# Softmax without division in an encoder layer: wide probabilities, and reciprocal sums multiplied into the gate

## The chip, the cores and the metric

The kernel runs on one core of a Trainium2 chip. The metric is the device time of one execution in microseconds. The core has five engines with an instruction queue each: TensorE (PE in the profile; PEld is its loading of weights), VectorE (DVE), ScalarE (ACT), GpSimd (POOL) and SyncE (SP). Every queue is worked off in order, and an instruction that waits holds up all that stand behind it. Transfers (DMAs) are issued by an instruction in one of the queues and then carried out by 16 DMA engines.

## The reference

One encoder layer on a sequence of 4096 tokens with 1024 channels: an input projection, windowed attention and a pooling branch, an output projection, and a normalised residual. Cut to what matters here:

```python
proj = jnp.einsum('bsd,de->bse', rmsnorm(x, pre_norm_g[l]), w_in[l])
q, k, v, g_a, u_p, g_p = jnp.split(proj, splits, axis=-1)
# banded_attention: blocks of 128 queries, keys of the block and of its two neighbours
s = jnp.where(valid, einsum(q, k) * scale + bias, NEG)
m = jnp.maximum(jnp.max(s, axis=-1, keepdims=True), sk)        # sk: one learned sink per head
p = jnp.exp(s - m)
p = p / (jnp.sum(p, axis=-1, keepdims=True) + jnp.exp(sk - m))
o = jnp.einsum('bnkgqs,bnskd->bnqkgd', p.astype(v.dtype), vw)
a = o * jax.nn.silu(g_a)
mixed = jnp.einsum('bse,ed->bsd', jnp.concatenate([a, pool], axis=-1), w_out[l])
x = x + rmsnorm(mixed, post_norm_g[l])
```

There are 8 query heads of 64 channels and 2 groups of keys and values. The division by the row sum can stand before the product with the values, or behind it.

## The kernel before, in words

Every float32 operand of a large product is carried as a pair of float16 numbers, a high part and a rest, and a product is three matmuls. The first stage (up to some 500 us of the span) projects the gates and the pooling branch and writes what the second stage needs to DRAM (`x_scr`, `ga_scr`, `yp_scr`, `w_scr`). The second stage is the attention with the output projection. It goes through the 32 blocks of 128 queries from the last to the first, in pairs: a unit `u` is the pair of blocks 2u + 1 (odd) and 2u (even), 256 tokens.

A block is attended in two halves of four heads. For one half:

- `scores` (L1313): TensorE multiplies queries and keys into two PSUM tiles `s`.
- `logits` (L1336), four times on VectorE: adds the bias, finds the row's minimum of the negated logits (`nm`), writes `p` in float32. GpSimd has put the sinks into one more column of `p` (L1330).
- `exps` (L1347), four times on ScalarE: the exponential over 384 + 1 columns, in place, with the row sum in `den`.
- `denominators` (L1354, L1357) on VectorE: divides the four sums by 2^14 and takes the reciprocals `rd`.
- `probs` (L1369), four times on ScalarE, one head each: the float16 high part of `p * rd`, into `pn`.
- `rests` (L1377), four times on VectorE: `p * rd` less that high part, also into `pn`.
- `turn` (L1386): a transposing DMA, issued by SP, from `pn` to `pt`.

When both halves of a block are turned, `values` (L1483, L1513) multiplies `pt` with the values `vv` on TensorE, `copy_o` (L1543, ScalarE) and `gate` (L1534, L1551, L1555, VectorE) apply a scale and the gate `ga` (loaded by `load_ga`, L1460, into tiles named `gb`), and the gated output `at` goes into the output projection.

That projection is done with seven products for two by two blocks of tokens and channels (`mix_p1` to `mix_p7`, `product` L1676). Their operands are sums and differences of `at` and of the pooling branch `yf` (`sum1` to `sum4`, L1611 to L1620), each split into a high part by ScalarE (`high`, L1578) and a rest by GpSimd (`low`, L1582), into tiles `y..` and `ys..`. Products are combined by VectorE (`add`, L1715), squared by ScalarE for the norm (`square`, L1699, output `jkb`), multiplied by the gain on GpSimd (`gain`, L1710), scaled (`mean`, L1728 and L1733, `residual`, L1737) and stored.

Between these stand the projections of the next unit's keys, values and queries (`project_t`, L1273). `do_q` projects the queries of a unit in two halves, both into the same PSUM bank `acc1`; `keep_q` (L1262 on ScalarE, L1263 on VectorE) copies each away before the bank is used again. Products also use that bank.

The order on every engine is written out by hand: `due(t, f, ...)` puts a step into a plan at a due time, and at the end all steps are issued in the order of their due times, each engine taking its own in that order. For blocks 27 to 2, 13 units, a loop (`for b in reversed(range(2, NB - 4))`) sets the due times; the four blocks before and the two behind have their times in tables (`soft(...)`, `at_(...)`). `softmax(b, half, t)` holds the offsets of the steps above:

```python
        for i in range(4):
            due(t + 0.1 + 0.67 * i, logits, b, half, i)
            due(t + 0.8 + 0.8 * i, exps, b, half, i)
            due(t + 4.5 + 0.6 * i, probs, b, half, i)
            due(t + 5.1 + 0.62 * i, rests, b, half, i)
        due(t + 4.3, denominators, b, half)
        due(t + 7.8, turn, b, half)
```

All DMAs are issued by SP. The DMAs share eight completion semaphores, taken in turn in the order of the plan, and a DMA is not issued before the one that had its semaphore last has landed.

Of the kernel before, what the change touches and what calls it, by code (L numbers as in the profile page):

```python
# [8 lines left out]
F32 = mybir.dt.float32  # L9
# [3 lines left out]
AF = mybir.ActivationFunctionType  # L13
ALU = mybir.AluOpType
# [3 lines left out]
P = 128  # L18
S = 4096
D = 1024  # L20
# [3 lines left out]
NB = S // P  # L24
BPM = T // P
NH = 8
# [27 lines left out]
P_SCALE = 2.0**14  # L54
# [80 lines left out]
def hybrid_layer(ctx: ExitStack, tc, io, out):  # L135
    nc = tc.nc
# [4 lines left out]
    dram = ctx.enter_context(tc.tile_pool(name="dram", bufs=1, space=DRAM))  # L141
    gemm = ctx.enter_context(tc.tile_pool(name="gemm", bufs=1, space=PSUM))

    XB0 = const.tile([P, 8192], F16, name="xb0")
# [35 lines left out]
    x_scr = dram.tile([NU, P, 2, 2, HK, UT], F16, name="x_scr")  # L180
    yp_scr = dram.tile([NB, P, 4, P], F32, name="yp_scr")
    ga_scr = dram.tile([NB, P, 4, P], F32, name="ga_scr")
    wb_scr = dram.tile([6, P, 2, D], F16, name="wb_scr")
    w_scr = dram.tile([8, P, 2, HK, 512], F16, name="w_scr")

# [25 lines left out]
    with ExitStack() as actx:  # L211
# [13 lines left out]
        rows = pa.tile([P, T], F32, name="rows")  # L225
# [728 lines left out]
        b = turn("n2")  # L954
# [322 lines left out]
                n += 1  # L1277

    pt, p_t, nm_t, den_t, rd_t, pn_t = {}, {}, {}, {}, {}, {}

    def keys(b):
        return [kb for kb in range(3) if 0 <= b - 1 + kb < NB]
# [6 lines left out]
    def due(t, fn, *args):  # L1289
        plan.append((t, len(plan), fn, args))  # L1290
# [30 lines left out]
    def logits(b, half, i):  # L1321

        kbs = keys(b)
        nk, lo, j0 = len(kbs) * P, kbs[0] * P, 2 * half
        if i == 0:
            nm_t[b, half] = pb.tile([P, 4], F32, name=f"nm{b}_{half}", tag="nm")
            den_t[b, half] = pb.tile([P, 4], F32, name=f"den{b}_{half}", tag="den")
            rd_t[b, half] = pb.tile([P, 4], F32, name=f"rd{b}_{half}", tag="rd")
            p = p_t[b, half] = pb.tile([P, 4, 3 * P + 1], F32, name=f"p{b}_{half}", tag="p")
            nc.gpsimd.tensor_copy(  # L1330
                p.rearrange("p (g j) k -> p g j k", g=2)[:, :, :, nk],
                nsink.rearrange("p (g j) -> p g j", g=2)[:, :, j0 : j0 + 2],
            )
        jj, gg = divmod(i, 2)
        hh, h = 2 * gg + jj, 4 * gg + j0 + jj
        nc.vector.tensor_tensor_reduce(  # L1336
            out=p_t[b, half][:, hh, :nk], in0=s_t[jj][:, gg, :nk],
            in1=bias[:, h, lo : lo + nk], scale=negc[:, h : h + 1], scalar=nsink[:, h : h + 1],
            op0=ALU.add, op1=ALU.min, accum_out=nm_t[b, half][:, hh : hh + 1],
        )  # L1340

    def exps(b, half, i):
        nk = len(keys(b)) * P
        jj, gg = divmod(i, 2)
        hh = 2 * gg + jj
        p = p_t[b, half]
        nc.scalar.activation(  # L1347
            p[:, hh, : nk + 1], p[:, hh, : nk + 1], AF.Exp, bias=nm_t[b, half][:, hh : hh + 1],
            scale=-1.0, accum_out=den_t[b, half][:, hh : hh + 1],
        )  # L1350

    def denominators(b, half):
        den = den_t.pop((b, half))
        nc.vector.tensor_scalar(  # L1354
            out=den, in0=den, scalar1=1.0 / P_SCALE, scalar2=None, op0=ALU.mult
        )
        nc.vector.reciprocal(rd_t[b, half], den)  # L1357

    def prob_view(b, half):
        nk = len(keys(b)) * P  # L1360
        return pn_t[b, half][:, : 8 * nk].rearrange("p (v h k) -> p v h k", v=2, h=4)

    def probs(b, half, i):
        nk = len(keys(b)) * P
        if i == 0:
            pn_t[b, half] = pb.tile(
                [P, 2 * 4 * 3 * P], F16, name=f"pn{b}_{half}", tag="pn", bufs=PN_BUFS
            )
        nc.scalar.activation(  # L1369
            prob_view(b, half)[:, 0, i], p_t[b, half][:, i, :nk], AF.Copy,  # L1370
            scale=rd_t[b, half][:, i : i + 1],
        )

    def rests(b, half, i):
        nk = len(keys(b)) * P
        pn4 = prob_view(b, half)
        nc.vector.scalar_tensor_tensor(  # L1377
            out=pn4[:, 1, i], in0=p_t[b, half][:, i, :nk], scalar=rd_t[b, half][:, i : i + 1],
            in1=pn4[:, 0, i], op0=ALU.mult, op1=ALU.subtract,
        )  # L1380

    def turn(b, half):
# [6 lines left out]
    def softmax(b, half, t):  # L1389

        for i in range(4):
            due(t + 0.1 + 0.67 * i, logits, b, half, i)
            due(t + 0.8 + 0.8 * i, exps, b, half, i)
            due(t + 4.5 + 0.6 * i, probs, b, half, i)
            due(t + 5.1 + 0.62 * i, rests, b, half, i)
        due(t + 4.3, denominators, b, half)
        due(t + 7.8, turn, b, half)


    kv_t = {}  # L1400
# [347 lines left out]
    def load_gain():  # L1748
        nc.sync.dma_start(
            gpost, io["g_post"].rearrange("(o a) -> o a", o=1).to_broadcast([P, D])  # L1750
        )

    now = [0.0]
    dummy = pb1.tile([P, 1], F32, name="dummy")

# [86 lines left out]
    def at_(t, fn, *args):  # L1842
        due(z + t, fn, *args)

    def soft(b, half, tl, te, td, tp, tr, tt):

        for i in range(4):
            at_(tl + 0.62 * i, logits, b, half, i)
            at_(te + 0.65 * i, exps, b, half, i)
            at_(tp + 0.55 * i, probs, b, half, i)  # L1850
            at_(tr + 0.62 * i, rests, b, half, i)
        at_(td, denominators, b, half)
        at_(tt, turn, b, half)

    def cast(th, tw, u, name, f, eng):
# [337 lines left out]
```

## Time and profile before

| what | before |
|---|---|
| median of 3 runs | 1161.81 us (1161.5 to 1165.42) |
| the profiled execution | 1162.76 us, span 1161.0 us |
| VectorE, ScalarE, GpSimd busy in the span | 947.8, 717.7, 313.7 us |
| HBM read, written | 114.68 MB, 60.34 MB |
| DMA packets | 301683, mean 197 GB/s |

The span runs from the first instruction to the last; the time of an execution holds some 1.8 us more around it. Rows of the timeline give the start, the duration, the engine, the line, the operation and its tiles; `x4` joins four in a row, and square brackets give the idle time ahead of an instruction and who ended it. `PEld` and `PE` overlap. Tile names are those of the code without their numbers. A row of the groups gives a line's engine and operation, its tiles and shapes, the count, the busy time in us and the mean of one in ns.

### The profile page before, as it was taken

How to read it: one execution, taken by the hardware profiler on the slowest of the kernel's cores; microseconds unless marked ns; L12 is line 12 of the kernel's file. 1: busy time of each engine (PE TensorE's matmuls, PEld its weight loads, DVE VectorE, ACT ScalarE, POOL GpSimd, SP SyncE). 2: the span in 40 equal slices, each digit the busy share in tenths (PEclk: the TensorE clock that was granted, in tenths of full speed). 3: DMA queues.
4: the chain of work that ended last, by engine and by line, in shares of the span. 5: the costliest groups of instructions: out<-in, count | busy, mean ns of one | idle time of the engine just before them, and what ended most of it. 6: DMA issues, size and time to landing. Idle time of an engine off the chain costs nothing. (4 is left out here: it accounts for less than half of the span.)

```text
span 1161.0 us, 32325 instructions
## 1 busy us (share of the span) xinstructions
PE 1146.3 (99%) x13420; PEld 873.5 (75%) x13420; DVE 947.8 (82%) x1875; ACT 717.7 (62%) x1485; POOL 313.7 (27%) x310
## 2 busy tenths in 40 slices
PE   8999999999999999999999999999999999999997
PEld 7998888888888888886667676576666767667653
DVE  6889988988799974568878888878887888887886
ACT  6876556536654542257676776676667677667772
POOL 0001120211111010201524433532533443353231
PEclk8999999999999999999999999999999999999999
DMA  9645575867667664299975886788777688777885
GB/s 344 217 128 180 174 259 183 285 229 238 227 190 225 206 179 134 76 289 242 250 185 144 197 211 143 200 202 177 177 196 184 148 198 215 140 196 165 178 216 143
DMA packets 301683, 228.36 MB, mean 197 GB/s; under 512 B 219568, under 2 KB 259504, under 8 KB 296928
## 3 DMA queue, kind: packets, MB, share of 16 engines
q1 hardware_dynamic: 301536, 226.30, 72.5%
q8 instruction: 105, 1.72, 0.6%
q14 instruction: 42, 0.34, 0.1%
HBM read 114.68 MB, written 60.34 MB: 151 GB/s over the span
## 5 line engine op out<-in xcount | busy, mean ns | idle before, releaser
L689 PEld LDWEIGHTS <-wq 128*128 128x128 f16 x4104 | 401.6, 98 | 50.4 <-DVE wq L310 2.6
L689 PE MATMUL y<-xt,wq 128*128 128x256 f16 x1512 | 203.3, 273 | 0.1
L1347 ACT ACTIVATE p<-p,nm 128x385 f32<-128x385 f32 (+1 forms) x256 | 152.9, 599 | 36.5 <-POOL p L1330 20.3
L1273 PE MATMUL aq<-xb,xb 128*128 128x256 f16 x1024 | 173.4, 273 | 0.2 <-DVE mo L1715 0.2
L1273 PEld LDWEIGHTS <-xb 128*128 128x128 f16 x1536 | 150.1, 98 | 26.4 <-issue 8.0
L1676 PE MATMUL ms<-wo,ys 128*128 128x512 f16 x720 | 163.7, 379 | 0.0
L1377 DVE SCALAR_TENSOR_TENSOR pn<-p,rd,pn 128x384 f16<-128x384 f32 (+1 forms) x256 | 157.6, 667 | 5.9 <-ACT pn L1369 5.9
L1336 DVE CUSTOM_DVE_ANT_0 p<-s,nt,nsink 128x384 f32<-128x384 f32 (+1 forms) x256 | 156.0, 666 | 2.0 <-PE s L1313 2.0
L1273 PE MATMUL aq<-xb,xt 128*128 128x256 f16 x512 | 139.6, 273 | 0.4 <-issue 0.4
L1369 ACT ACTIVATE pn<-p,rd 128x384 f16<-128x384 f32 (+1 forms) x256 | 134.8, 596 | 4.4 <-issue 1.1
L307 POOL TENSOR_TENSOR yt<-yt,sg 128x512 f32<-128x512 f32 (+2 forms) x32 | 51.0, 1594 | 301.6 <-DVE yt L310 214.8
L1676 PEld LDWEIGHTS <-ys 128*128 128x128 f16 x720 | 68.1, 98 | 83.9 <-POOL ys L1582 4.8
L1676 PE MATMUL m<-wo,y 128*128 128x512 f16 x540 | 121.8, 379 | 0.0
L1676 PEld LDWEIGHTS <-y 128*128 128x128 f16 x540 | 51.4, 98 | 63.5 <-ACT at L1543 2.9
L1273 PE MATMUL kv<-xb,xb 128*128 128x256 f16 x512 | 86.7, 273 | 0.0
L1710 POOL TENSOR_TENSOR mo<-mo,gpost 128x512 f32<-128x512 f32 x39 | 63.7, 1634 | 84.4 <-ACT jkb L1699 83.2
L1273 PEld LDWEIGHTS <-xt 128*128 128x128 f16 x768 | 75.1, 98 | 10.6 <-issue 0.8
L689 PE MATMUL plain<-xb,wq 128*128 128x256 f16 x576 | 68.0, 276 | 2.1 <-DVE wq L310 2.0
L1273 PE MATMUL kv<-xb,xt 128*128 128x256 f16 x256 | 69.8, 273 | 0.0
L689 PE MATMUL v<-xt,wq 128*128 128x256 f16 x504 | 68.6, 273 | 0.1
L689 PE MATMUL v<-xb,wq 128*128 128x256 f16 x504 | 68.6, 273 | 0.0
L689 PE MATMUL y<-xb,wq 128*128 128x256 f16 x504 | 68.6, 273 | 0.0
(221 smaller groups left out, 1854.3 us busy)
## 6 DMA issues: line engine op xcount, KB each, us to landing
nt<-in_xT SPq DMA_DIRECT2D x28, 512.0 KB
x_scr<-xb SPq DMA_DIRECT2D x14, 1024.0 KB
xb<-x_scr SPq DMA_DIRECT2D x14, 1024.0 KB
xr<-in_x SPq DMA_DIRECT2D x28, 512.0 KB
out<-xr SPq DMA_DIRECT2D x28, 512.0 KB
xn<-in_x SPq DMA_DIRECT2D x27, 512.0 KB
ga_scr<-cc SPq DMA_DIRECT2D x64, 128.0 KB
raw<-in_w_out SPq DMA_DIRECT2D x16, 512.0 KB
```

The costliest lines, as they stand in the source:

```text
L307: eng.tensor_tensor(out=out, in0=in0, in1=in1, op=op)
L689: nc.tensor.matmul(b[:, s], wq[:, slot[q, op], wv, s, k, :], x[:, xv, k, :], start=(first and k + s + wv + xv == 0), stop=(last and k == H ...
L1273: nc.tensor.matmul(acc, w[:, j, k, :], x[:, kh, v, kt, :], start=(n == 0), stop=(n == 3 * KT - 1),)
L1336: nc.vector.tensor_tensor_reduce(out=p_t[b, half][:, hh, :nk], in0=s_t[jj][:, gg, :nk], in1=bias[:, h, lo : lo + nk], scale=negc[:, h : h ...
L1347: nc.scalar.activation(p[:, hh, : nk + 1], p[:, hh, : nk + 1], AF.Exp, bias=nm_t[b, half][:, hh : hh + 1], scale=-1.0, accum_out=den_t[b, ...
L1369: nc.scalar.activation(prob_view(b, half)[:, 0, i], p_t[b, half][:, i, :nk], AF.Copy, scale=rd_t[b, half][:, i : i + 1],)
L1377: nc.vector.scalar_tensor_tensor(out=pn4[:, 1, i], in0=p_t[b, half][:, i, :nk], scalar=rd_t[b, half][:, i : i + 1], in1=pn4[:, 0, i], op0= ...
L1676: nc.tensor.matmul(z_t[u, tag], y[:, k, yi, :], wo[o][:, wi, k, :], start=(n == 0 and acc is None), stop=(n == 3 * HK - 1), skip_group_che ...
L1710: eng.tensor_tensor(out=mo, in0=mo, in1=gpost[:, cs], op=ALU.mult)
```

## The change

The probabilities are no longer divided. `probs` writes the float16 part of `p * 2^14` for two heads in one operation of up to 768 columns, and `rests` likewise. The division moves behind the product with the values: for each block, when all eight row sums are there (`den` is now one tile for both halves), VectorE takes the reciprocals of all eight (`rec[0]`) and transposes them in blocks of 32 (`rec[1]`); ScalarE issues four DMAs that store the rows to DRAM (`keep_rows`, `rd_scr`) and, later, two that load them back, each spread over 64 partitions (`load_rows`, into `rdb`, a free part of the tile `XB0`, with room for two blocks); GpSimd multiplies them into the gate tile in place (`divide`), and `gate` is as it was. The due times of `probs`, `rests` and `turn` change with it.

```diff
+    rec = [pb1.tile([P, 32], F32, name=f"rec{i}") for i in range(2)]
+    rdb = XB0[:, 6 * D :].bitcast(F32).rearrange("p (i h q) -> p i h q", i=2, h=4)
...
             p[:, hh, : nk + 1], p[:, hh, : nk + 1], AF.Exp, bias=nm_t[b, half][:, hh : hh + 1],
-            scale=-1.0, accum_out=den_t[b, half][:, hh : hh + 1],
+            scale=-1.0,
+            accum_out=den_t[b][:, 4 * gg + 2 * half + jj : 4 * gg + 2 * half + jj + 1],
         )
 
-    def denominators(b, half):
-        den = den_t.pop((b, half))
-        nc.vector.tensor_scalar(
-            out=den, in0=den, scalar1=1.0 / P_SCALE, scalar2=None, op0=ALU.mult
-        )
-        nc.vector.reciprocal(rd_t[b, half], den)
+    def denominators(b):
+        nc.vector.reciprocal(rec[0][:, :NH], den_t.pop(b))
+        nc.vector.transpose(out=rec[1], in_=rec[0])
+
+    def keep_rows(b):
+        for i in range(4):
+            nc.scalar.dma_start(
+                rd_scr[b, :, 32 * i : 32 * i + 32], rec[1][32 * i : 32 * i + NH, :]
+            )
+
+    def load_rows(b):
+        for g in range(2):
+            rows = rd_scr[b, 4 * g : 4 * g + 4, :].rearrange("(o h) q -> o h q", o=1)
+            nc.scalar.dma_start(
+                rdb[64 * g : 64 * g + 64, b % 2], rows.to_broadcast([64, 4, P])
+            )
+
+    def divide(b):
+        ga = ga_t[b]
+        nc.gpsimd.tensor_tensor(out=ga, in0=ga, in1=rdb[:, b % 2], op=ALU.mult)
...
-        nc.scalar.activation(
-            prob_view(b, half)[:, 0, i], p_t[b, half][:, i, :nk], AF.Copy,
-            scale=rd_t[b, half][:, i : i + 1],
-        )
+        hs = slice(2 * i, 2 * i + 2)
+        nc.scalar.mul(prob_view(b, half)[:, 0, hs], p_t[b, half][:, hs, :nk], P_SCALE)
...
+        hs = slice(2 * i, 2 * i + 2)
         nc.vector.scalar_tensor_tensor(
-            out=pn4[:, 1, i], in0=p_t[b, half][:, i, :nk], scalar=rd_t[b, half][:, i : i + 1],
-            in1=pn4[:, 0, i], op0=ALU.mult, op1=ALU.subtract,
+            out=pn4[:, 1, hs], in0=p_t[b, half][:, hs, :nk], scalar=P_SCALE,
+            in1=pn4[:, 0, hs], op0=ALU.mult, op1=ALU.subtract,
         )
...
-            due(t + 4.5 + 0.6 * i, probs, b, half, i)
-            due(t + 5.1 + 0.62 * i, rests, b, half, i)
-        due(t + 4.3, denominators, b, half)
-        due(t + 7.8, turn, b, half)
+        for i in range(2):
+            due(t + 4.1 + 0.75 * i, probs, b, half, i)
+            due(t + 5.0 + 0.95 * i, rests, b, half, i)
+        if half:
+            due(t + 4.3, denominators, b)
+            due(t + 5.5, keep_rows, b)
+            due(t + 9.6, load_rows, b)
+            due(t + 15.0, divide, b)
+        due(t + 6.9, turn, b, half)
```

The tables ahead of the loop and behind it (`soft`) get the same steps, with `keep_rows` at `max(td + 0.4, tp + 0.9)`, `load_rows` at `max(tp, td) + 4.0` and `divide` at `max(tt + 2.6, tp + 7.5, td + 7.5)`.

What stands in a row now, at two places of the loop. ScalarE first, from the second half of an odd block (23) to the first half of the even block behind it. Before (`pn_1` and `p_1` belong to the second half of the odd block, `p_0`, `q_0` and `pn_0` to the first half of the even block and its queries; `ys` are high parts for the products):

```order
L1369 ACTIVATE pn_1_10184<-p_1_10152,rd_1_10151 128x384 x4
L1578 CAST ys_11_10226<-at_10078 128x4x128
L1578 CAST ys_11_10228<-s_11_10132 128x4x128
L1699 ACTIVATE jkb_00_10280,ss_10180<-m_11_10164 128x512
L1578 CAST ys_11_10283<-yf_11_9570 128x4x128
L1347 ACTIVATE p_0_10338,den_0_10336<-p_0_10338,nm_0_10335 128x385 x4
L1262 ACTIVATE q_0_10352<-aq_0_10285 128x512
L1369 ACTIVATE pn_0_10355<-p_0_10338,rd_0_10337 128x384 x4
```

The same place now (`rd_scr<-rec` are the four stores, `xb<-rd_scr` the two loads):

```order
L1388 ACTIVATE pn_1_10113<-p_1_10087 128x768
L1362 DMA rd_scr<-rec_6088 8x32 x4
L1600 CAST ys_11_10161<-at_10015 128x4x128
L1369 DMA xb_66<-rd_scr 64x512 x2
L1600 CAST ys_11_10165<-s_11_10069 128x4x128
L1721 ACTIVATE jkb_00_10217,ss_10117<-m_11_10099 128x512
L1600 CAST ys_11_10220<-yf_11_9518 128x4x128
L1350 ACTIVATE p_0_10274,den_10273<-p_0_10274,nm_0_10272 128x385 x4
L1388 ACTIVATE pn_0_10287<-p_0_10274 128x768
L1263 ACTIVATE q_0_10289<-aq_0_10222 128x512
L1388 ACTIVATE pn_0_10287<-p_0_10274 128x768
```

Six DMAs have come in, on both sides of the first cast, the loads wait for the stores, and one of the two wide probabilities now stands ahead of `q_0`.

GpSimd, in the even block that follows, from the low part of the odd block's output to the low parts of the pooling branch. Before (`mo` are gains, `rs` the norm's power, `p` the copies of the sinks):

```order
L1582 TENSOR_TENSOR y_10_10496<-at_10438,y_10_10496 128x4x128
L1710 TENSOR_TENSOR mo_1_10179<-mo_1_10179,gpost 128x512
L1330 COPY p_0_10677<-nsink 128x4
L1710 TENSOR_TENSOR mo_1_10179<-mo_1_10179,gpost 128x512
L1733 TENSOR_TENSOR rs_1_10715<-ms_1_10713,mhalf 128x1
L1710 TENSOR_TENSOR mo_0_10178<-mo_0_10178,gpost 128x512
L1733 TENSOR_TENSOR rs_0_10759<-ms_0_10757,mhalf 128x1
L1582 TENSOR_TENSOR y_10_10762<-yf_10_10224,y_10_10762 128x4x128
```

The same place now (`gb<-gb,xb` is the multiplication by the loaded rows):

```order
L1604 TENSOR_TENSOR y_10_10427<-at_10371,y_10_10427 128x4x128
L1732 TENSOR_TENSOR mo_1_10116<-mo_1_10116,gpost 128x512
L1333 COPY p_0_10607<-nsink 128x4
L1732 TENSOR_TENSOR mo_1_10116<-mo_1_10116,gpost 128x512
L1755 TENSOR_TENSOR rs_1_10645<-ms_1_10643,mhalf 128x1
L1375 TENSOR_TENSOR gb_10483<-gb_10483,xb_66 128x512
L1732 TENSOR_TENSOR mo_0_10115<-mo_0_10115,gpost 128x512
L1755 TENSOR_TENSOR rs_0_10685<-ms_0_10683,mhalf 128x1
L1604 TENSOR_TENSOR y_10_10689<-yf_10_10159,y_10_10689 128x4x128
```

The multiplication has come in ahead of the gain of the first half, of its norm and of the low part `y`, and it waits there for the loads.

More of the change, by code (lines that the diff above doesn't have):

```diff
@@ L182, in hybrid_layer @@
     ga_scr = dram.tile([NB, P, 4, P], F32, name="ga_scr")
+    rd_scr = dram.tile([NB, NH, P], F32, name="rd_scr")
     wb_scr = dram.tile([6, P, 2, D], F16, name="wb_scr")
@@ L1326, in logits @@
             nm_t[b, half] = pb.tile([P, 4], F32, name=f"nm{b}_{half}", tag="nm")
-            den_t[b, half] = pb.tile([P, 4], F32, name=f"den{b}_{half}", tag="den")
-            rd_t[b, half] = pb.tile([P, 4], F32, name=f"rd{b}_{half}", tag="rd")
+            if half == 0:
+                den_t[b] = pb.tile([P, NH], F32, name=f"den{b}", tag="den")
             p = p_t[b, half] = pb.tile([P, 4, 3 * P + 1], F32, name=f"p{b}_{half}", tag="p")
@@ L1751, in load_gain @@
         )
+    due(-1.0, nc.vector.memset, rec[0], 0.0)
     now = [0.0]
@@ L1849, in soft @@
             at_(te + 0.65 * i, exps, b, half, i)
-            at_(tp + 0.55 * i, probs, b, half, i)
-            at_(tr + 0.62 * i, rests, b, half, i)
-        at_(td, denominators, b, half)
+        for i in range(2):
+            at_(tp + 0.8 * i, probs, b, half, i)
+            at_(tr + 0.95 * i, rests, b, half, i)
+        if half:
+            at_(td, denominators, b)
+            at_(max(td + 0.4, tp + 0.9), keep_rows, b)
+            at_(max(tp, td) + 4.0, load_rows, b)
+            at_(max(tt + 2.6, tp + 7.5, td + 7.5), divide, b)
         at_(tt, turn, b, half)
```

## The prediction

> **What bounds the kernel now.** I read the page's first part, then the stretches, then the timeline of one period of the attention loop, engine by engine. The page and two stretches, one of the loop and one of the end (columns: length, then busy time of PE, PEld, DVE, ACT and POOL, the granted clock, the DMA share and GB/s):
>
> ```profile
> PE 1146.3 (99%) x13420; PEld 873.5 (75%) x13420; DVE 947.8 (82%) x1875; ACT 717.7 (62%) x1485; POOL 313.7 (27%) x310
> 500.00:1100.00 600.00, 597.71 (x8270) 403.71 (x8268) 494.64 (x1129) 414.68 (x1023) 231.79 (x237) 1.00 0.82 190
> 1100.00:1161.00 61.00, 53.50 (x543) 26.23 (x541) 48.10 (x103) 29.89 (x81) 15.70 (x17) 0.99 0.69 189
> ```
>
> TensorE is idle for 600 - 597.71 = 2.3 us of the 600 us in which the changed code runs, at full clock, and for 7.5 us in the last 61. The change touches no matmul, so its whole possible gain is those 9.8 us, and part of the 7.5 is the drain behind the last matmul. Freed time on VectorE or ScalarE is worth nothing in the loop; lost time costs as soon as it is larger than the slack in front of some matmul. So the question is where that slack is small. TensorE's own rows:
>
> ```profile
> 605.52 0.93 PE L1313 MATMUL s<-k_all,q 64*32 64x288 f16 x48
> 646.85 0.93 PE L1313 MATMUL s<-k_all,q 64*32 64x288 f16 x48
> 677.13 0.93 PE L1313 MATMUL s<-k_all,q 64*32 64x288 f16 x48
> 677.99 0.28 PE L1273 MATMUL aq<-xb,xb 128*128 128x256 f16 x1
> ```
>
> One period (an odd block `o`, then the even block `e = o - 1`) is 646.85 - 605.52 = 41.33 us, and the loop has 13 of them. At 677.99 the second query projection of the period starts. Its accumulator `acc1` is that of the first one, so it waits until ScalarE and VectorE have copied that away (`keep_q`, L1262 and L1263). ScalarE and VectorE ahead of it:
>
> ```profile
> 664.52 0.60 ACT L1347 ACTIVATE p<-p,nm 128x385 f32<-128x385 f32 x1
> ...
> 665.12 0.56 ACT L1694 COPY mo<-m 128x512 f32<-128x512 f32 x1
> 665.71 2.13 ACT L1369 ACTIVATE pn<-p,rd 128x384 f16<-128x384 f32 x4
> 667.75 0.60 ACT L1578 CAST ys<-at 128x512 f16<-128x512 f32 x1
> 668.92 0.62 ACT L1578 CAST ys<-s 128x512 f16<-128x512 f32 x1 [0.57 <-PE m L1676]
> 670.20 0.60 ACT L1699 ACTIVATE jkb<-m 128x512 bf16<-128x512 f32 x1 [0.67 <-DVE mo L1704]
> ...
> 670.79 0.61 ACT L1578 CAST ys<-yf 128x512 f16<-128x512 f32 x1
> 672.80 0.62 ACT L1347 ACTIVATE p<-p,nm 128x385 f32<-128x385 f32 x1 [1.40 <-POOL p L1330]
> ...
> 675.21 0.57 ACT L1262 ACTIVATE q<-aq 128x512 f16<-128x512 f32 x1
> 675.82 0.69 DVE L1263 SCALAR_TENSOR_TENSOR q<-aq,q 128x512 f16<-128x512 f32 x1
> 717.49 0.69 DVE L1263 SCALAR_TENSOR_TENSOR q<-aq,q 128x512 f16<-128x512 f32 x1
> 718.46 0.93 PE L1313 MATMUL s<-k_all,q 64*32 64x288 f16 x48
> ```
>
> The copy ends at 675.82 + 0.69 = 676.51, **1.48 us** before TensorE wants the bank; one period later it ends at 718.18 and the scores, which take 677.99 - 677.13 = 0.86, start at 718.46, so 719.32 - 718.18 = **1.14 us**. In the 7.68 us from 665.12 to 672.80 ScalarE is idle for 0.57 + 0.67 + 1.40 = 2.6 us. The 1.40 is a chain: the last cast, then GpSimd's low half of it, then its copy of the sinks, which the exponentials need:
>
> ```profile
> 671.48 1.16 POOL L1582 TENSOR_TENSOR ys<-yf,ys 128x512 f16<-128x512 f32 x1 [0.37 <-ACT ys L1578]
> 672.58 0.31 POOL L1330 COPY p<-nsink 128x4 f32<-128x4 f32 x2
> ```
>
> **The change, part by part.** Wider probabilities and rests first. The groups by shape, with their mean ns:
>
> ```profile
> L1377 DVE SCALAR_TENSOR_TENSOR pn<-p,rd,pn 128x384 f16<-128x384 f32 x240 | 150.3, 677 | 4.0 <-ACT pn L1369 4.0
> L1369 ACT ACTIVATE pn<-p,rd 128x384 f16<-128x384 f32 x240 | 128.0, 603 | 3.1 <-issue 1.1 <-ACT p L1347 1.0 <-ACT k_all L1262 0.2
> L1369 ACT ACTIVATE pn<-p,rd 128x256 f16<-128x256 f32 x16 | 6.8, 497 | 1.3 <-DVE rd L1357 0.8 <-ACT jkb L1699 0.4
> ```
>
> On ScalarE 128 columns cost 603 - 497 = 106 ns, so an operation of 768 columns takes 603 + 3 x 106 = 0.92 us, and about 0.83 from start to start (neighbours overlap by 0.1: four in 2.13). Two end after 1.75 where four ended after 2.13: 0.38 us a half are freed. VectorE gains by the same reasoning a tenth or two per half, and the half's division by `P_SCALE` and one reciprocal become one reciprocal and one 32-column transpose a block. None of this is worth time in the loop, since TensorE covers it. It can shorten the last 61 us, by nothing or by some 3 of the 7.5; I take 1.
>
> Then the six DMAs a block on ScalarE. The trace has no DMA on that engine. The nearest rows are two like shapes on SP, small stores out of a 32-column transposed tile and a broadcast load, with the time their issue takes:
>
> ```profile
> 185.29 2.11 SPq L459 DMA_DIRECT2D rs_scr<-turned  x4
> L466 SPq DMA_DIRECT2D rows<-rs_scr x5: 327/392/647, 158.3 to 354.4; - x5
> 0.72 1.82 SPq L131 DMA_DIRECT2D xb<-in_x  x4
> 3.37 0.63 ACT L417 ACTIVATE nt<-xb 128x512 f32<-128x512 f32 x1 [1.15 <-DMA xb<-in_x]
> ```
>
> Four stores hold the issuing queue 2.11 us and two loads about 0.9 (0.39 each and a gap). Below, the cost could be nothing, if ScalarE issues beside its arithmetic; above, 2.11 + 2 x 0.65 = 3.4 by the slowest load. I take 2.11 + 0.9 = 3.0, the nearest rows. The Trainium skill ("DMA: Bandwidth & Descriptors", Anatomy of one DMA) puts the sequencer's share of an issue at about 50 ns, which would make the six 0.3 us and bring the no-change case below; the rows of SP, at 0.39 to 0.53 each, speak against it, and no run here has shown ScalarE.
>
> The load has to wait until the stores have landed. A 256 KB load issued at 0.72 was there at 3.37, 2.65 us later on idle DMA. A store has 1 KB, so 2.65 is the upper bound and nothing the lower; I take 1.65 from its beginning, 1.1 after its issue ends. With nothing the loads would go 0.5 earlier than below, with 2.65 they would go 1.0 later.
>
> Now the odd half, put together. Second probabilities end at 665.12 + 0.83 + 0.59 (the copy) + 0.83 = 667.37. Four stores: 669.5. First cast: 670.1. The loads wait until 670.6, issue until 671.5. Second cast: 672.1. Square: 672.7. Third cast: 673.3. Against 671.40 that is 1.9 late, and with GpSimd's unchanged 1.40 the exponentials start at 674.7. Behind them the new order puts one wide probability ahead of `q`: 0.83 more. So the bank comes free 1.9 + 0.83 = **2.7 us** later, with 1.14 to 1.48 of slack: a stall of 1.2 to 1.6, I take 1.4. The even half has the same order, a wide probability before `q`, and the bank's next user is the second of two products:
>
> ```profile
> 641.58 5.34 PE L1676 MATMUL ms<-wo,ys 128*128 128x512 f16 x24
> 642.43 0.69 DVE L1263 SCALAR_TENSOR_TENSOR q<-aq,q 128x512 f16<-128x512 f32 x1
> ```
>
> The second begins half of 5.34 after 641.58, at 644.25, and the copy ends at 643.12: 1.1 of slack, of which 0.83 goes, and the half now also starts late by what the odd half could not catch up. I take a stall of 0.4, between 0 and 0.6. In the even half the stores and loads fall where ScalarE waits for sums that come from TensorE anyway.
>
> GpSimd's multiplication stands, for the even block, ahead of work that TensorE needs soon:
>
> ```profile
> 651.46 0.54 POOL L1733 TENSOR_TENSOR rs<-ms,mhalf 128x1 f32<-128x1 f32 x1 [1.65 <-DVE den L1354]
> 656.19 0.85 POOL L1733 TENSOR_TENSOR rs<-ms,mhalf 128x1 f32<-128x1 f32 x1 [1.74 <-DVE ms L1728]
> 657.01 2.27 POOL L1582 TENSOR_TENSOR y<-yf,y 128x512 f16<-128x512 f32 x2
> 658.27 1.04 PE L1676 MATMUL m<-wo,y 128*128 128x512 f16 x4
> L1710 POOL TENSOR_TENSOR mo<-mo,gpost x39: 1269/1357/2357, 563.1 to 1066.0; 128x512 f32<-128x512 f32 x39
> ```
>
> It enters after 652.0 and takes 1.3 to 2.4 us (the range of the multiplication by `gpost`, of the same shape); the idle 1.74 ahead of 656.19 hides it if the rows have landed by then. I cost it at nothing; if they land later, each microsecond reaches `y` and the product at 658.27 almost whole.
>
> **Sum.** The profiled execution took 1162.76 us with a span of 1161.0; the median of the runs shown is 1161.81, a microsecond less. 13 periods x (1.4 + 0.4) = 23.4. Six blocks before and after the loop, three periods' worth of 0 to 1.8 each: 2, and 1 off at the end. 1162.76 + 23.4 + 2 - 1 = 1187; against the median the same within 1.
>
> **The rivals.**
> *No change.* ScalarE's issues cost it little, or its queue runs ahead, so that the 2.6 us of idle time take them in, and the bank comes free within its slack: shift 0.83 at most. Then 1160 to 1167. For it: the bound of nothing is not excluded by any row. Against it: each piece on SP holds its queue, and 3.0 is more than 2.6.
> *Queueing behind the transposes.* SP spends several microseconds on each transposing DMA:
>
> ```profile
> 669.03 3.65 SPq L1386 DMA_TRANSPOSE pt<-pn  x1
> ```
>
> The probabilities of the same half are ready just when ScalarE issues. If only one queue can issue at a time, the loads wait until about 673.2 instead of 670.6: 2.6 more at the bank, and in the even half up to 3.65 in front of the copy of the attention output, of which ScalarE's idle time takes about two. 1.4 + 0.4 + 2.6 + 1.4 = 5.8 a period, 1162.76 + 75 = 1238. The Trainium skill states such a rule: "Perfetto Trace Analysis", DMA Instruction, HWDGE, has descriptor generation locked for one sequencer at a time. No run here shows it, as all DMAs are SP's.
> *Rows late for the multiplication.* If loads land 2 us later than 2.65 after their issue, behind other traffic (the DMA share of the loop is 0.82), GpSimd's in-order queue holds `y` up: 1 to 2 us a period beside the main stall, 1175 to 1205.
> *Faster.* This end needs the tail: VectorE and ScalarE work of blocks 1 and 0 sits between products there, and if half of the 7.5 us went and the loop kept its pace, 1158; over 0.5% would need 5.8 us, so nearly all of it.
>
> **How the numbers follow.** Main forecast, 1187 (its own range 1172 to 1205): 0.45. Transposes, 1205 to 1245: 0.22. Late rows: 0.08. No change: 0.22. Faster by more than 0.5% (5.8 us, about what a measurement of this kernel can tell): 0.03. Slower is 0.45 + 0.22 + 0.08 = 0.75. The range runs from 1162, which leaves out the faster and the lower part of the no-change case (0.10), to 1235, which leaves out the upper part of the transposes (0.09).
>
> **What would show it.** Right: a TensorE wait at L1273's `aq` for VectorE of 1 to 2 us in each period, a period near 43.1, the third cast and the exponentials behind it about 2 us later in the period, and DMA issues on ScalarE of 0.4 to 0.5 us. Transposes: issues on ScalarE of 2 us and more beside an SP transpose. No change: the period still 41.3 and issues that take no time between two ScalarE operations. Late rows: GpSimd waiting for a DMA at the multiplication, and TensorE for `y`.

## The result and the profile after

The changed kernel takes 1215.3 us (median, 1207.8 to 1218.8), the kernel before 1162.1 in the same runs: a ratio of 1.044 (95% interval 1.039 to 1.050), 53 us slower. Forecast were 1187 and a range of 1162 to 1235. The profiled execution took 1212.5 with a span of 1210.7 us, 49.7 more than before.

The page's first row of the kernel after, then two stretches (length, busy time of PE, PEld, DVE, ACT, POOL, granted clock, DMA share, GB/s):

```profile
PE 1154.8 (95%) x13420; PEld 873.1 (72%) x13420; DVE 928.0 (77%) x1684; ACT 674.7 (56%) x1357; POOL 358.7 (30%) x342
...
500.00:1100.00 600.00, 567.65 (x7663) 379.03 (x7661) 441.74 (x882) 348.06 (x841) 250.60 (x246) 0.99 0.83 191
1100.00:1210.70 110.70, 95.52 (x1148) 53.74 (x1146) 81.01 (x156) 53.48 (x135) 41.86 (x40) 0.99 0.71 174
```

TensorE, idle for 2.3 of these 600 us before, is now idle for 32.4. ScalarE and VectorE are less busy than before and the kernel is slower: the time is waits, not work. What TensorE waited for from 490 us on (sum, times, longest):

```profile
PE m L1698 <- DVE vs L1264: 8.7, 9, 1.4
PE o L1535 <- DMA pt<-pn: 7.6, 6, 1.8
PE m L1698 <- POOL y L1604: 5.7, 6, 2.2
PE o L1505 <- DMA pt<-pn: 4.6, 3, 3.3
PE p L1505 <- DVE q L1264: 3.9, 1, 3.9
```

The wait forecast at the second query projection is not among them. The loss is spread over the program. The same two scores, those of the 13th and the 59th half of a block (the first halves of blocks 25 and 2), serve as marks in every run. They enclose 11.5 of the loop's 13 periods; the loop's first period lies ahead of them and its last block behind. Before, these stand in the timeline of TensorE at 605.52 and at

```profile
1082.70 0.93 PE L1313 MATMUL s<-k_all,q 64*32 64x288 f16 x48
```

and after at

```profile
618.06 0.93 PE L1316 MATMUL s<-k_all,q 64*32 64x288 f16 x48
1125.65 0.93 PE L1316 MATMUL s<-k_all,q 64*32 64x288 f16 x48
```

So of the 49.7 us, 12.5 are lost before the first mark, 30.4 between the marks (11.5 periods of 41.5 that now take 44.1) and 6.7 behind the second.

Where a period loses its time is read best in the even half. First the chain that ended last (start, us, what; pieces under 0.1 us left out), followed through one such place:

```profile
746.03 0.21 DVE rec L1357
746.27 0.22 DVE rec L1358
746.51 0.29 ACTq L1362
746.80 0.35 ACT q L1263
747.15 0.35 ACT pn L1388
747.54 5.62 DMA rd_scr<-rec
753.34 0.45 ACTq L1369
753.83 0.71 ACTq L1369
754.71 0.47 issue
...
762.71 0.34 DVE k_all L1264
763.08 0.38 ACT vs L1263
```

and ScalarE's own timeline there:

```profile
747.19 0.76 ACTq L1362 DMA_DIRECT2D rd_scr<-rec  x2
750.90 0.63 ACT L1721 ACTIVATE jkb<-mo 128x512 bf16<-128x512 f32 x1 [2.96 <-DVE mo L1737]
...
753.34 1.20 ACTq L1369 DMA_DIRECT2D xb<-rd_scr  x2
754.64 0.63 ACT L1721 ACTIVATE jkb<-mo 128x512 bf16<-128x512 f32 x1 [3.01 <-DVE nm L1339]
...
755.27 0.60 ACT L1350 ACTIVATE p<-p,nm 128x385 f32<-128x385 f32 x1
```

The four stores are issued by 747.95. The first load is issued at 753.34, 5.4 us later, when 4 KB have landed. Behind it in ScalarE's queue stand a square and the next half's exponentials, which start 755.27 - 751.10 = 4.2 us after their scores; before the change that took 1.5. (The name "DVE nm" in the bracket is the last semaphore on the profile's list; the chain names the DMA.) In the odd half the same two steps cost ScalarE nothing to speak of:

```profile
728.63 0.31 ACTq L1362 DMA_DIRECT2D rd_scr<-rec  x1
728.91 0.84 ACT L1388 ACTIVATE pn<-p 128x768 f16<-128x768 f32 x1
728.98 0.65 ACTq L1362 DMA_DIRECT2D rd_scr<-rec  x2
729.67 0.62 ACT L1600 CAST ys<-at 128x512 f16<-128x512 f32 x1
730.62 1.12 ACTq L1369 DMA_DIRECT2D xb<-rd_scr  x2
731.85 0.62 ACT L1600 CAST ys<-s 128x512 f16<-128x512 f32 x1 [1.55 <-PE m L1698]
```

The issues run beside ScalarE's arithmetic, the loads come 1.0 us after the stores, and ScalarE would have waited for TensorE until 731.85 anyway. TensorE loses something in the odd blocks all the same: in five of them, between the marks, it waited 6.0 us in all for transposed probabilities (`o` for `pt`; 0.2 before). There the row loads go out within 0.7 us of the start of the transposing DMA.

### The profile page after: what moved, and what is told of

It reads as the page before. It is cut to its first block, busy times and chain, and to the rows that moved or that the text cites. A ratio compares the mean times of both kernels' runs of the same rounds, so it can differ in the third digit from the quotient of the medians.

```text
span 1210.7 us, 32380 instructions
## 1 busy us (share of the span) xinstructions
PE 1154.8 (95%) x13420; PEld 873.1 (72%) x13420; DVE 928.0 (77%) x1684; ACT 674.7 (56%) x1357; POOL 358.7 (30%) x342
## 4 chain that ended last, share of the span: by engine, by line
PE 30%; ACT 15%; DVE 11%; DMA 9%; issue 4%; ACTq 2%; POOL 2%; SPq 0%; DVEq 0%; POOLq 0%
ACT p L1350 7%; PE y L690 7%; PE aq L1274 5%; DMA rd_scr<-rec 5%; PE v L690 4%; DMA pt<-pn 3%; PE m L1698 3%; DVE pn L1394 3%; PE ms L1698 2%; ACT pn L1388 2%; PE kv L1274 2%; PE x L690 2%; ACTq L1369 2%; DVE at L1577 2%; PE s L1316 1%
## 5 line engine op out<-in xcount | busy, mean ns | idle before, releaser
L1394 DVE SCALAR_TENSOR_TENSOR pn<-p,pn 128x768 f16<-128x768 f32 (+1 forms) x128 | 136.4, 1098 | 24.5 <-ACT pn L1388 24.5
L1698 PE MATMUL m<-wo,y 128*128 128x512 f16 x540 | 125.9, 384 | 17.1 <-DVE vs L1264 8.7
L1388 ACT ACTIVATE pn<-p 128x768 f16<-128x768 f32 (+1 forms) x128 | 102.3, 817 | 0.0
L1732 POOL TENSOR_TENSOR mo<-mo,gpost 128x512 f32<-128x512 f32 x39 | 56.7, 1453 | 114.1 <-ACT jkb L1721 114.1
L1264 DVE SCALAR_TENSOR_TENSOR q<-aq,q 128x512 f16<-128x512 f32 x31 | 21.4, 692 | 71.6 <-ACT q L1263 71.6
L1375 POOL TENSOR_TENSOR gb<-gb,xb 128x512 f32<-128x512 f32 x32 | 46.7, 1458 | 82.2 <-DMA xb<-rd_scr 68.2
```

The costliest lines, as they stand in the source:

```text
L1375: nc.gpsimd.tensor_tensor(out=ga, in0=ga, in1=rdb[:, b % 2], op=ALU.mult)
L1388: nc.scalar.mul(prob_view(b, half)[:, 0, hs], p_t[b, half][:, hs, :nk], P_SCALE)
L1394: nc.vector.scalar_tensor_tensor(out=pn4[:, 1, hs], in0=p_t[b, half][:, hs, :nk], scalar=P_SCALE, in1=pn4[:, 0, hs], op0=ALU.mult, op1=ALU ...
L1698: nc.tensor.matmul(z_t[u, tag], y[:, k, yi, :], wo[o][:, wi, k, :], start=(n == 0 and acc is None), stop=(n == 3 * HK - 1), skip_group_che ...
L1732: eng.tensor_tensor(out=mo, in0=mo, in1=gpost[:, cs], op=ALU.mult)
```

## The experiments

All times are medians; the kernel before took 1161.9 to 1162.8 beside them. "Loop" is the time between the two marks, "ahead" what lies before the first and "behind" after the second, from each run's profiled execution. The four runs of the change lie between 1207.8 and 1218.8 us, so a difference to it is known to some 7 us either way.

| kernel | us | ratio to before | ahead | loop | behind |
|---|---|---|---|---|---|
| before | 1162.1 | | 605.5 | 477.2 | 78.3 |
| e1: no stores, no loads, no multiplication | 1161.6 | 0.999 (0.998 to 1.000) | 604.6 | 479.4 | 76.7 |
| e7: multiplication alone, early | 1162.0 | 1.000 (0.999 to 1.002) | 604.5 | 479.5 | 76.7 |
| e8: multiplication alone, on VectorE | 1168.6 | 1.005 (1.004 to 1.007) | 603.7 | 485.9 | 77.7 |
| e2: multiplication alone | 1174.8 | 1.011 (1.009 to 1.013) | 603.8 | 491.2 | 77.7 |
| e9: and the stores | 1176.5 | 1.012 (1.011 to 1.014) | 607.1 | 491.3 | 77.8 |
| e10: multiplication and loads that wait for nothing | 1190.9 | 1.025 (1.024 to 1.027) | 615.8 | 491.5 | 83.4 |
| e11: and the stores | 1190.9 | 1.025 (1.024 to 1.027) | 615.2 | 493.8 | 79.8 |
| e12: all, but the multiplication does not use the rows | 1204.1 | 1.036 (1.033 to 1.039) | 613.6 | 507.0 | 82.1 |
| the change | 1215.3 | 1.044 (1.039 to 1.050) | 618.1 | 507.6 | 85.0 |
| e4: the change, three loads of SP earlier | 1203.6 | 1.036 (1.033 to 1.038) | 616.9 | 500.4 | 83.1 |
| e6: e4, row loads moved | 1204.5 | 1.035 (1.031 to 1.039) | 622.5 | 502.2 | 82.1 |
| e13: e4, multiplication later | 1207.4 | 1.039 (1.036 to 1.041) | 620.8 | 503.9 | 81.0 |
| e5: loads from the input x, no wait | 1216.9 | 1.047 (1.046 to 1.049) | 619.4 | 516.7 | 82.2 |
| e3: row loads issued by SP | 1233.3 | 1.061 (1.059 to 1.062) | 622.3 | 527.4 | 80.9 |

**e1, the wide operations alone.**

```diff
-            due(t + 5.5, keep_rows, b)
-            due(t + 9.6, load_rows, b)
-            due(t + 15.0, divide, b)
```

(and the same three lines in `soft`)

> Leaves out the four stores, the two loads and the multiplication of every block; the wide probabilities, their new order, the reciprocal and its transpose stay (the output lacks the division by the sums). Theory A (the stores land late and ScalarE's queue stands at the loads until they have): all of the loss goes, 1158 to 1168 us, and the period is 41.3 to 41.6. Theory B (the rows come late for the multiplication, and GpSimd's queue stands there): the same, 1158 to 1168. Theory C (the multiplication itself, 1.3 to 2.4 us of GpSimd that also slows VectorE): the same. Theory D (the wide operations and their new order): 1190 or more, the period still 43 or more.

1161.6 us. The wide operations and their order cost nothing and bring nothing in sum (2.2 us more between the marks, 2.5 less outside them): theory D falls. It is also the floor of this change: with the whole transport free it would equal the kernel before, since TensorE was idle for 2.3 of 600 us there. No later version was faster.

**e2, the multiplication alone.**

```diff
-            due(t + 5.5, keep_rows, b)
-            due(t + 9.6, load_rows, b)
+    due(20.0, nc.vector.memset, rdb, 1.0)
```

> Leaves out the stores and loads, keeps the multiplication on GpSimd in its place, with rows of ones written once. A and B: 1158 to 1172 us, period 41.3 to 41.9. C: 1185 or more, with VectorE's wide rests still at 1.7 us in the even half and TensorE's product of y waiting over 1 us.

1174.8: 13.2 us above e1, between the two expectations, and 1.0 us a period (42.6 for 41.6). The reason stands in the timelines of GpSimd and VectorE. In e2:

```profile
693.99 1.27 POOL L1375 TENSOR_TENSOR gb<-gb,xb 128x512 f32<-128x512 f32 x1
```

```profile
694.06 2.28 DVE L1757 SCALAR_TENSOR_TENSOR xr<-mo,rs,xr 128x1024 f32<-128x1024 f32 x1 [0.65 <-POOL rs L1753]
```

and VectorE in e1:

```profile
692.93 1.28 DVE L1756 SCALAR_TENSOR_TENSOR xr<-mo,rs,xr 128x1024 f32<-128x1024 f32 x1 [0.65 <-POOL rs L1752]
```

The residual sum on VectorE takes 2.28 us beside the multiplication and 1.28 without it. The rests, the keys (`k_all`) and `ms` queue behind it, so `y` and the next product come 1.0 us later. GpSimd's queue had room, as the forecast said; the multiplication was paid on VectorE. The Trainium skill ("SBUF — State Buffer", SBUF: two separate sides) says that these two engines hold a shared pair of ports for a whole instruction. An estimate by that rule is 1.20 us lost, from 694.06 to the end of the multiplication at 695.26; the row shows 1.00, so it agrees in the main.

Here the multiplication begins 0.07 us ahead of the sum. In the change it waits for its rows and begins behind it:

```profile
757.24 1.28 DVE L1759 SCALAR_TENSOR_TENSOR xr<-mo,rs,xr 128x1024 f32<-128x1024 f32 x1 [1.57 <-POOL rs L1755]
758.50 1.27 POOL L1375 TENSOR_TENSOR gb<-gb,xb 128x512 f32<-128x512 f32 x1 [1.29 <-DMA xb<-rd_scr]
```

So the sum takes 1.28 us between the marks of the change, and of e3, e4, e5, e10, e11 and e13; it takes 2.28 in e2, e9 and e12 and in most periods of e6. The 13.2 us are the price of the multiplication at its planned place. What it costs in the change, where it comes later, no run isolates.

**e7, the multiplication early, and e8, on VectorE.** Both without stores and loads.

```diff
-            due(t + 15.0, divide, b)
+            due(t + (15.0 if b % 2 else 6.0), divide, b)
```

(and `load_ga` of the even blocks 8.5 us earlier, as in e4 below)

> The kernel with the multiplication alone (rows of ones, no stores and no loads), the even block's multiplication moved 9 us ahead in GpSimd's queue, into its idle 7 us before the gains by gpost, and the gate's input loaded earlier for it. If the 1.0 us a period that the multiplication costs comes from its place ahead of y: 1160 to 1166 us. If it comes from GpSimd and VectorE hindering each other wherever it stands: 1170 or more.

```diff
-        nc.gpsimd.tensor_tensor(out=ga, in0=ga, in1=rdb[:, b % 2], op=ALU.mult)
+        nc.vector.tensor_tensor(out=ga, in0=ga, in1=rdb[:, b % 2], op=ALU.mult)
```

> The kernel with the multiplication alone, on VectorE instead of GpSimd, in the same place of the plan: 0.7 us at the rate of the gate's own multiplication. If GpSimd's queue was what delayed y: 1160 to 1168 us. If VectorE's own queue at that place (rests, low halves) is as tight: 1172 or more.

1162.0: in its early place, where both engines have room, the multiplication is free. GpSimd in e7 (start, us):

```profile
681.28 1.28 POOL L1375 TENSOR_TENSOR gb<-gb,xb 128x512 f32<-128x512 f32 x1
```

It is a question of place alone; but the real rows cannot be there at that time, which is just behind the half whose sums they hold. On VectorE the time is 1168.6, 0.4 us more than e1 in most periods, between the two expectations. The residual sum takes 2.28 us there too: the multiplication ahead of it in VectorE's queue makes it begin at 694.58, 0.07 us behind a gain of GpSimd (694.51), where in e1 it began 0.06 us ahead of that gain.

**e9, e10 and e11: stores, and loads that wait for nothing.** e9 leaves `load_rows` out, e10 `keep_rows`; in e10 and e11 the loads read a fixed copy:

```diff
+    rd_in = dram.tile([NH, P], F32, name="rd_in")
+    due(-1.0, nc.sync.dma_start, rd_in, io["x"][0:NH, 0:P])
-            rows = rd_scr[b, 4 * g : 4 * g + 4, :].rearrange("(o h) q -> o h q", o=1)
+            rows = rd_in[4 * g : 4 * g + 4, :].rearrange("(o h) q -> o h q", o=1)
```

> The changed kernel without the two row loads of a block: the stores stay on ScalarE, the multiplication stays on GpSimd with rows of ones written once. It holds no wait for a landing and 1 KB a store. If the stores' issue on ScalarE is dear (the first block's four took 2.3 us and ScalarE stood for 2.2): 1185 or more. If they run beside arithmetic as in the loop (0.3 us each): 1174 to 1181, near the 1174.8 without them.

> The changed kernel without the stores: the loads read one fixed copy of eight rows in DRAM, contiguous as the real rows are, so they never wait. If the loads' issue, their traffic beside the transposes, and their own landing time before the multiplication are the cost: 1190 to 1210 us, with GpSimd waiting 1 us and more for the rows in most blocks and TensorE for transposed probabilities. If only the wait for the stores cost: 1174 to 1181.

> Stores and loads both, but the loads read the fixed contiguous copy and never wait for a store; unlike the run from the input x, whose rows lie apart and took 19456 packets, the packets are those of the changed kernel (7168). If the packets made that run slow: 1190 to 1203 us. If loads that come earlier run into the transposing DMAs and that is as dear as the wait: 1208 to 1220 again. If the wait was the whole cost of the rows: 1174 to 1184.

The stores cost 1176.5 - 1174.8 = 1.6 us in all, no more than the runs scatter: 128 issues on ScalarE are almost free. Issue times of the change (engine, operation, count, ns min/median/max):

```profile
L1362 ACTq DMA_DIRECT2D rd_scr<-rec x128: 269/306/2034, 508.7 to 1184.9; - x128
L1369 ACTq DMA_DIRECT2D xb<-rd_scr x64: 452/530/1697, 518.1 to 1187.6; - x64
```

Loads that wait for nothing cost 14.4 to 16.1 us, with the stores or without, and nearly all of it outside the loop, 8 to 12 us ahead of it and 2 to 6 behind; there TensorE waited 14.0 us for transposed probabilities in e10 (the longest 5.3). Between the marks they cost 0.3 (e10) and 2.5 (e11), but that is a balance: the loads also move the multiplication off the residual sum, which is back at 1.28 us, and that may hide a cost of about the same size. The wait for the stores is the rest: 1215.3 - 1190.9 = 24.5 us, 13.8 of it in the loop. The sum takes 1.28 us in e11 and in the change alike, so this step is the clean one. It is seen on ScalarE: the exponentials behind the even block's loads start 2.1 us after their scores in e11 and 3.7 in the change (means of twelve periods). Together: 13.2 + 1.6 + 14.4 + 24.5 = 53.7, against e1; these are steps in one order and not independent parts.

**e12, which queue the wait acts through.**

```diff
-        nc.gpsimd.tensor_tensor(out=ga, in0=ga, in1=rdb[:, b % 2], op=ALU.mult)
+        g = gpost[:, : 4 * P].rearrange("p (h q) -> p h q", h=4)
+        nc.gpsimd.tensor_tensor(out=ga, in0=ga, in1=g, op=ALU.mult)
```

> The changed kernel with all stores, loads and waits in place, but the multiplication on GpSimd takes its second operand from the gain that lies in SBUF all along, so that it never waits for the rows (the output is multiplied by the gain where it should be by the reciprocals). Runs so far: multiplication alone 1174.8, with stores 1176.5, with stores and loads that wait for nothing 1190.9, the changed kernel 1215.3 us. If the last step is ScalarE's queue standing at the loads: 1203 to 1216. If it is GpSimd standing at the multiplication for late rows, with the copy of the sinks and y behind it: 1178 to 1192.

1204.1. GpSimd never waits for the rows here, and in the change it did so 21 times:

```profile
POOL gb L1375 <- DMA xb<-rd_scr: 68.2, 21, 9.2
```

Taking that away gives back 11.2 us in the medians and 8.0 in the profiles: 4.4 ahead of the loop, 3.0 behind it and 0.6 in it. In the loop two effects work against each other: GpSimd no longer stands, but the multiplication is again 0.07 us ahead of the residual sum, which takes 2.28. So what GpSimd's standing costs in the loop is not separated. For ScalarE the run to compare is e9 (491.3), where GpSimd does not stand either and the sum takes the same 2.28; e12 (507.0) adds the loads and their wait, 15.7 us. ScalarE in e12:

```profile
747.64 0.63 ACT L1722 ACTIVATE jkb<-mo 128x512 bf16<-128x512 f32 x1 [2.95 <-DVE mo L1738]
750.31 1.11 ACTq L1369 DMA_DIRECT2D xb<-rd_scr  x2
751.52 0.63 ACT L1722 ACTIVATE jkb<-mo 128x512 bf16<-128x512 f32 x1 [3.16 <-DVE nm L1339]
```

So in the loop ScalarE's in-order queue, standing at the loads, is enough for a loss of this size without GpSimd. Not all of the 15.7 is the standing: 6.1 us are TensorE's waits for transposed probabilities in four odd blocks, as in the change. GpSimd's standing at the multiplication is seen outside the loop.

**e4 and e3: what holds the landing up, and moving the loads to SP.**

```diff
-        due(t0 + 10.0, load_ga, b)
+        due(t0 + (10.0 if b % 2 else 1.5), load_ga, b)
-            due(t0 + 9.0, load_xr, u + 1, 1)
-            due(t0 + 9.0, load_xr, u + 1, 0)
+            due(t0 + 1.0, load_xr, u + 1, 1)
+            due(t0 + 1.0, load_xr, u + 1, 0)
```

> The changed kernel with three loads of SP, 1.25 MB, that stand just ahead of the even block's stores (the residual's input twice, the gate's input) issued some 9 us earlier. If that traffic is why the stores land 5 us after their issue: they land within 2.5 us, the loads issue at least 2 us earlier, and the time falls to 1175 to 1195 us. If the transposing DMAs or the way a landing is reported are why: the landing still takes 4 to 5.5 us and the time stays within 1203 to 1222.

1203.6, so 11.7 us less (expected were 20 to 40). By its time e4 lies at the edge of the second branch, by the landing in neither. In the change these loads, 1.25 MB, are issued as the stores begin (746.51):

```profile
745.46 1.01 SPq L1745 DMA_DIRECT2D xr<-in_x  x2
746.52 0.42 SPq L1482 DMA_DIRECT2D gb<-ga_scr  x1
```

With them out of the way the even block's row loads go out 3.0 to 3.6 us after the stores in the loop, where it was 3.6 to 5.5 (4.3 on the mean of twelve) in the change, and the exponentials behind them start 2.4 us after their scores and not 3.7. Now a square ahead of the loads in ScalarE's queue decides, not the landing:

```profile
742.68 0.85 ACTq L1362 DMA_DIRECT2D rd_scr<-rec  x2
746.41 0.63 ACT L1721 ACTIVATE jkb<-mo 128x512 bf16<-128x512 f32 x1 [2.96 <-DVE mo L1737]
746.57 0.45 ACTq L1369 DMA_DIRECT2D xb<-rd_scr  x1
```

e6 below, with the same early loads of SP, has the row loads directly behind the stores, and there they go out after 1.0 to 1.7 us, with SP's transposing DMAs still in place. So traffic ahead of them is why a few KB land late. Some of e4's periods are at 42.5, e2's length; four others carry 0.5 to 2.0 us of waits for transposed probabilities.

```diff
-            nc.scalar.dma_start(
+            nc.sync.dma_start(
                 rdb[64 * g : 64 * g + 64, b % 2], rows.to_broadcast([64, 4, P])
```

> The changed kernel with the two loads of a block issued by SP, in the same place of the plan; the stores stay on ScalarE. A: ScalarE no longer stands there, the exponentials of the next half start 2 us after its scores and not 4, and half or more of the loss goes: 1172 to 1195 us. B: the rows come no earlier, so GpSimd still waits 3 us and more at the multiplication, and 1200 to 1216 us remain. If SP then holds its own transposes: above 1216.

1233.3: the third branch. SP's queue holds the transposes and reaches the loads late (4.9 to 7.5 us after the stores in the loop), and GpSimd stands longer:

```profile
POOL gb L1375 <- DMA xb<-rd_scr: 143.6, 28, 14.3
```

TensorE then waited 33.6 us for `y`. An in-order queue that holds urgent work is a poor place for a dependent load, whichever engine's it is.

**e6 and e13: versions that should have been better.** Both compute everything and start from e4.

```diff
-            due(t + 9.6, load_rows, b)
+            due(t + (9.6 if b % 2 else 7.0), load_rows, b)
-            at_(max(tp, td) + 4.0, load_rows, b)
-            at_(max(tt + 2.6, tp + 7.5, td + 7.5), divide, b)
+            at_(rows_at[b][0], load_rows, b)
+            at_(rows_at[b][1], divide, b)
```

> A version that should be better, computing everything: the three loads of SP early as in the run before, and the row loads moved to where they are not waited for: in the loop's even half directly behind the stores (ahead of a square that waits for TensorE's sum anyway), before and after the loop some 4 to 5 us later, with the multiplication 3 us behind them. If waiting for landings in ScalarE's queue is the cost: 1176 to 1190 us. If traffic or issue is: 1200 or more.

```diff
-            due(t + 15.0, divide, b)
+            due(t + (15.0 if b % 2 or b == 2 else 19.8), divide, b)
```

> A version that computes everything: the three loads of SP early, and the even block's multiplication placed in GpSimd's queue behind the low half of y that the next product needs, ahead of the other. If the multiplication's place is the 1.0 us a period that the run with it alone showed, and its wait for the rows reaches y there: the loop's period falls from 42.5 to 44.2 before to 41.6 to 43, and the time from 1203.6 to 1186 to 1195 us. If the transposes that the loads delay set the period: 1198 to 1206.

1204.5 and 1207.4: neither is better than e4, and e13 lies above both of its ranges. In e6 ScalarE no longer stands in the loop, but with the rows there in time the multiplication is back 0.07 us ahead of the residual sum, which takes 2.28 us in ten of twelve periods (1.28 in e4); TensorE also waits 8.1 us for transposed probabilities, and ahead of the loop the profiled execution, which took 1208.6, is 5.6 us worse. A version with e6's loads and the multiplication begun just behind the sum was not run. In e13 the multiplication, begun at 766.46 for 1.27 us, misses the residual sum as in e4 and meets the gate in every period. VectorE:

```profile
767.76 1.63 DVE L1577 TENSOR_TENSOR at<-at,gb 128x512 f32<-128x512 f32 x1 [0.34 <-POOL gb L1375]
```

The gate's product waits 0.34 for it and takes 1.63, where it takes 0.71 in e1 and 0.7 to 1.6 in e4; the low half of `y` that follows on GpSimd runs beside it. The microsecond moved; it did not go.

**e5, a first try at e11** that read rows of the input x.

```diff
-            rows = rd_scr[b, 4 * g : 4 * g + 4, :].rearrange("(o h) q -> o h q", o=1)
+            rows = io["x"][4 * g : 4 * g + 4, 0:P].rearrange("(o h) q -> o h q", o=1)
```

> The changed kernel with everything in place, stores, loads and multiplication, but the loads read rows of the input x that lie in DRAM all along, so they never wait for the stores (the gate is multiplied by values of x in place of the reciprocal sums). If the wait for the landing of the stores is what the rows cost: 1172 to 1184 us, near the 1174.8 with the multiplication alone, and the stretch before the loop as long as there (its mark at 604, not 618). If the traffic and the issues themselves cost, or the transposing DMAs suffer from them: 1195 or more.

1216.9, and it would have spoken against the wait as a cause. But rows of x lie 4 KB apart, and ScalarE's DMA queue moved the same bytes in more packets (queue: packets, MB, share), in e5

```profile
q10 hardware_dynamic: 19456, 8.53, 4.8%
```

and in e11

```profile
q10 hardware_dynamic: 7168, 8.53, 4.0%
```

With the packets of the change, e11 answers the question: 26 us less than e5.

**What stays open.** In e4, e6 and e13 the loop is still 9 to 13 us above e2's, and the waits named there are in part for transposed probabilities (`o` for `pt`: 8 to 15 us in all, 5.3 to 7.7 between the marks, all in odd blocks). Whether the transposes are late because ScalarE's issues come between SP's, or because the row loads share the DMA engines with them, was not separated. e10 shows none of it in the loop, and there the odd block's loads go out 3.4 us ahead of the transposing DMA; in e11 it is 1.0 to 1.6 us ahead (0.4 us of waits), in the change 0.7 ahead to 0.4 behind (6.0 us). What GpSimd's standing costs in the loop is open too.

## Why the prediction was wrong in size

*TensorE has no slack, so the gain is nothing.* Right: e1 is 0.999 of before.

*The six issues hold ScalarE 3.0 us a block.* Wrong. A store takes 0.31 us to issue and a load 0.53 (medians), beside ScalarE's arithmetic; e9 prices 128 stores at 1.6 us. The 50 ns that the forecast quotes from the Trainium skill is the sequencer's share alone; the shortest whole issue here took 0.27 us. The rows of SP were the nearest, but the true value lay near the lower bound, nothing.

*The odd half stalls 1.4 us a period at the second query projection.* This carried 18 of the 24 us of the sum and did not occur: that wait shows once, 1.2 us, ahead of the marks. The landing was sized right there (loads 0.9 to 2.1 us after the last issue, 1.2 on the mean, 1.1 taken), and without the issues' 3.0 us the slack of 1.14 to 1.48 took in the rest.

*"In the even half the stores and loads fall where ScalarE waits for sums that come from TensorE anyway."* This is the step that failed: they do fall there, but the loads can go out only 3.6 to 5.5 us after the stores, not 1.1, since 1.25 MB of SP's loads are issued at the same time; 2.65, measured on idle DMA engines, was no upper bound for a DMA share of 0.8 to 1.1 (744 to 752 us). What stands behind the loads is then late: squares, exponentials, keys, `y`. The forecast put this at nothing; the runs show 24.5 us for the wait, 13.8 of it in the loop (e11 against the change).

*The even half's wide probability ahead of `q`, 0.4 a period.* Not seen at `q`: e1 has no such wait between the marks, though its periods are some 0.2 us longer than before. *The end, 1 us off.* About right: the stretch behind the second mark is 1.6 us shorter in e1.

*The multiplication is hidden by 1.74 us of idle GpSimd.* GpSimd had the room, but at the planned place VectorE pays 1.00 us a period, 13.2 in all (e2, e7). In the change the rows come too late for that: the sum keeps its 1.28 us, and the gate takes 0.9 to 1.6 where it took 0.8. The forecast's own row had the sign, 1269 to 2357 ns for one shape on GpSimd, and took it as a range of GpSimd alone.

*Six blocks outside the loop: 2 us.* The stretches outside the marks cost 12.5 and 6.7, and the loop's first period and last block are in them. By the first scores of block 27, where the loop begins, 5.4 us are lost, and from those of block 1 on 4.9. Ahead of the loop the DMA share was over 1 already before (1.05 to 1.17 from 500 to 580 us) and rows came up to 9.2 us late. e11 (loads that do not wait) and e12 (a multiplication that does not) are still 11.4 and 9.8 us above e2 at the first mark; which engine's standing counts there is open.

*The rivals.* "No change" had the issues right and the rest wrong. "Queueing behind the transposes" is not what happened: ScalarE's issues go out while SP issues a transpose (a pair of loads from 818.07 to 819.45 inside one from 818.02 to 822.17), and the transposes take 3.99 us in the loop's median, 3.88 before. "Rows late for the multiplication" is real: 11.2 us by e12, most of it outside the loop.

So the direction, slower, came from a mechanism that did not act, and was right by luck. The measured time came from three terms that were put at nothing or 2: the landing in the even half, the multiplication, and the blocks outside the loop.

## What to carry to other kernels

A store and a dependent load through DRAM cost the landing under the traffic of that very moment, and the engine whose in-order queue holds the load stands for it: read the landing from a busy stretch, list what stands behind the load, and move large transfers from just ahead of the store. An operation on GpSimd has to be checked against what VectorE does at that moment, not only against GpSimd's own idle time; which of the two begins first, by 0.07 us, decided here who paid. And where the bounding engine is busy for 99.6% of the stretch, freed work elsewhere brought nothing, and what the change added could only lose.

## What the runs showed of the hardware

After a wait of a few microseconds TensorE can run at half clock for a while. In the change, TensorE stood for 3.87 us until 524.42; two stretches around its end (length, busy time of PE and the others, then granted clock, DMA share and GB/s):

```profile
522.00:526.00 4.00, 1.58 (x31) 1.58 (x32) 4.00 (x8) 2.04 (x5) 1.40 (x2) 0.58 0.39 77
526.00:530.00 4.00, 4.00 (x29) 1.90 (x25) 3.06 (x10) 3.54 (x9) 0.00 (x0) 0.56 1.21 179
```

Busy at about half clock for 1.58 us and at 0.56 for 4: an estimated 0.8 + 1.8 = 2.6 us of work lost on top of the wait, and the clock fell in the same way after a wait of 3.32 us until 581.63. A wait of 2.02 us until 951.03 in e4 brought the clock to 0.50:

```profile
950.00:952.00 2.00, 0.97 (x27) 0.97 (x30) 2.00 (x3) 0.53 (x1) 1.08 (x1) 0.82 1.02 342
952.00:954.00 2.00, 2.00 (x64) 1.25 (x56) 1.86 (x2) 0.69 (x1) 1.38 (x2) 0.50 1.05 409
```

The Trainium skill ("TensorE: Matmul & The Clock Gate", HAM oscillation — how this bites in real kernels) describes this halving and advises against gaps over some 3.4 us; here it came after 2.0. The length of the wait does not settle it: in e3 the clock stayed at 1.00 after a wait of 2.93 us until 866.11. The forecast had no term for it.
